# Attention by pairs of heads in the hybrid stages of a four-layer network on one NeuronCore

## The chip, the cores and the metric

The kernel runs as one program on one core of a Trainium2 chip. The metric is the device time of that core in microseconds. TensorE (PE in the profile) multiplies matrices and transposes, VectorE (DVE) and ScalarE (ACT) do elementwise work and move results out of PSUM, GpSimd (POOL) does a little, and SyncE (SP) issues the weight loads. Each engine executes its own queue strictly in the order in which the program was written.

## The reference

A sequence of 256 tokens of width 1024 passes eight stages: retention, dense FFN, stick-breaking attention, mixture of experts, and then twice a hybrid mixer followed by a convolutional FFN. Only the two hybrid mixers matter here. Cut to that:

```python
def hybrid_mixer(hn, w_in, conv_w, conv_b, gate_b, head_g, w_out):
    aq, ak, av, mq, mk, mv, mo, gates = split(hn @ w_in)      # 3 x 512, 4 x 512, 16 columns
    q, k = apply_rotary(heads(aq, 8)), apply_rotary(heads(ak, 8))
    attn = dilated_attention(q, k, heads(av, 8))              # 8 heads of 64: softmax(q k^T / 8 + bias) v
    mq, mk = split(silu(depthwise_conv_centred([mq, mk], conv_w, conv_b)))
    hm = mlstm(mq, mk, mv, gates) + flip(mlstm(flipped))      # 4 heads of 128, gates by scans over the tokens
    hm = hm * rsqrt(mean(hm * hm) + eps)
    return concat(attn, hm * head_g * sigmoid(mo)) @ w_out
```

The kernel folds the three dilation patterns into one additive bias (the log of how many patterns admit a pair of tokens), so each head is one softmax over 256 keys.

## The kernel before

All products are made in three passes of fp32r: each weight and activation is split in a high and a low part. A weight unit is a tile of 128 x 2048. It arrives by DMA (`raw`), ScalarE copies it to its high part `wh` (L83), VectorE subtracts to get the low part `wl` (L94). `W.advance()` issues the splits that buffers allow, five pairs at most; `W.get()` hands the oldest pair to the matmuls.

A hybrid stage (`hybrid`) goes through 14 input units, u = 0 to 13, and then four output units (`tail`). Each input unit is a projection of 48 matmuls (`mm3`, L200). Units 0 to 3 give queries and keys of the attention; `rotated` (L1012 on) turns them by angle on VectorE and `flip` (L1023 on) transposes them on TensorE, ScalarE copying the result to `qk`. Behind unit 3 `gating` computes the mLSTM gates with scans on VectorE (L981 to L999). Units 4 and 8 give attention values. Units 5, 6, 9 and 10 give mLSTM queries and keys, with a convolution of five taps (`conv` and `taps`: L1152 on ScalarE, eight instructions of L1159 on VectorE, a tanh L1162, `silu` L1166). Units 7 and 11 give mLSTM values, 12 and 13 the output gate.

The rest is tucked in behind the projections by the unit's number. Before the change, `attend(n)` handles one head per unit in u = 4 to 12: TensorE transposes the previous head's probabilities (L1041) and makes this head's scores (L1046), VectorE adds the bias and takes maxima (L1055), ScalarE exponentiates (L1061). `normalise` (L1065, L1067) follows the taps of the same unit, ahead of the mLSTM work in `todo` and ahead of `W.advance()`. `pv` (L1074) makes the value products of a pair of heads at u = 7, 9, 11, 13. `todo` places the mLSTM work: gate matrices (`gates`, L1089 and L1100), scores (`mscores`, L1106 and L1111), products and their norms (`mout`, L1127 to L1146).

PSUM has four single-bank buffers (`psP`) and two double-bank buffers (`psA`); an instruction that writes one waits until its last reader is done. The program's order is written by hand; no scheduler moves anything.

Of the kernel before, what the change touches and what calls it, by code (L numbers as in the profile page):

```python
# [10 lines left out]
F32 = mybir.dt.float32  # L11
# [4 lines left out]
AF = mybir.ActivationFunctionType  # L16
OP = mybir.AluOpType
PSUM = bass.MemoryType.PSUM

S, D = 256, 1024  # L20
# [105 lines left out]
def tok(t):  # L126
    return slice(t * 128, t * 128 + 128)
# [6 lines left out]
class Net:  # L134
# [805 lines left out]
    def hybrid(self, l, joint0):  # L940
        nc, tc, a, W = self.nc, self.tc, self.a, self.W
        with tc.tile_pool(name="h1", bufs=1) as p, tc.tile_pool(name="h2", bufs=2) as w:
# [66 lines left out]
            at = p.tile([128, 4, 2, S], F32, tag="at", name="at")  # L1009
            dn = {}  # L1010

            def rotated(ps):  # L1012

                x = w.tile([128, 2, 4, 2, 32], F32, tag="cv", name="ro")
                t1, t2 = (w.tile([128, 2, 8, 32], F32, tag="wk", name=n) for n in ("t1", "t2"))
                for t, i in ((t1, 0), (t2, 1)):
                    nc.vector.tensor_tensor(t, ps.rearrange("p t (h d) -> p t h d", d=32),  # L1017
                                            cs[:, :, i, None, :].to_broadcast([128, 2, 8, 32]), op=OP.mult)
                t1, t2 = (t.rearrange("p t (h i) d -> p t h i d", i=2) for t in (t1, t2))
                nc.vector.tensor_tensor(x[:, :, :, 0, :], t1[:, :, :, 0, :], t2[:, :, :, 1, :], op=OP.subtract)  # L1020
                nc.vector.tensor_tensor(x[:, :, :, 1, :], t2[:, :, :, 0, :], t1[:, :, :, 1, :], op=OP.add)
                return x.rearrange("p t h i d -> p t (h i d)")
# [8 lines left out]
                else:  # L1031
                    nc.scalar.activation(dst[0], ps, AF.Copy, scale=scale)

            def attend(n):

                A = self.psA()
                if n > 0:
                    x = at[:, (n - 1) % 2]
                    for jt in range(2):
                        for it in range(2):  # L1040
                            nc.tensor.transpose(A[:, 0, jt * S + it * 128:jt * S + it * 128 + 128], x[:, it, tok(jt)],  # L1041
                                                self.ident)
                r = slice(64 * (n % 2), 64 * (n % 2) + 64)
                ps = A[:, 1, :].rearrange("p (t s) -> p t s", t=2)
                for t in range(2 if n < 8 else 0):
                    nc.tensor.matmul(ps[:, t, :], lhsT=qk[r, 0, n // 2, tok(t)], rhs=qk[r, 1, n // 2, :],  # L1046
                                     start=True, stop=True)
                if n > 0:
                    nc.scalar.activation(at[:, 2 + (n - 1) % 2], A[:, 0, :].rearrange("p (t s) -> p t s", t=2), AF.Copy)
                if n == 8:  # L1050
                    return
                x = at[:, n % 2]
                m = self.small(2, "m")
                for t in range(2):
                    nc.vector.tensor_tensor_reduce(x[:, t, :], ps[:, t, :], bias[:, t, :], 1.0, -3e38, op0=OP.add,  # L1055
                                                   op1=OP.max, accum_out=m[:, t:t + 1])
                nm = self.small(2, "nm")
                nc.vector.tensor_scalar(nm, m, -1.0, None, op0=OP.mult)
                dn[n] = d = self.small(2, "dn")
                for t in range(2):  # L1060
                    nc.scalar.activation(x[:, t, :], x[:, t, :], AF.Exp, bias=nm[:, t:t + 1], accum_out=d[:, t:t + 1])  # L1061

            def normalise(n):
                d = dn.pop(n)
                nc.vector.reciprocal(d, d)  # L1065
                x = at[:, n % 2]
                nc.vector.tensor_tensor(x, x, d[:, :, None].to_broadcast([128, 2, S]), op=OP.mult)  # L1067

            def pv(c):
                ps = self.psP([128, S])  # L1070
                for j in range(2):
                    hd = slice((2 * c + j) * 64, (2 * c + j) * 64 + 64)
                    for jt in range(2):
                        nc.tensor.matmul(ps[64 * j:64 * j + 64, :], lhsT=v[:, jt, hd], rhs=at[:, 2 + j, jt, :],  # L1074
                                         start=(jt == 0), stop=(jt == 1), skip_group_check=True)
                self.split(ya[0][:, c, :], ya[1][:, c, :], ps)
# [38 lines left out]

            def mout(h):
                x = Dt.pop(h)
                A = [self.psP([128, 2, 129]) for _ in range(2)]

                def o(i, t):  # L1120
                    return A[i][:, t, :]

                def vv(t):
                    return va[:, t, h, :]

                def mm(out, l, r, start, stop):
                    nc.tensor.matmul(out, lhsT=l, rhs=r, start=start, stop=stop)  # L1127

                mm(o(0, 0), x[:, 0, 0:128], vv(0), True, True)
                mm(o(0, 1), x[:, 0, 128:256], vv(0), True, False)  # L1130
                mm(o(0, 1), x[:, 0, 256:384], vv(1), False, True)
                mm(o(1, 0), x[:, 1, 0:128], vv(0), True, False)
                mm(o(1, 0), x[:, 1, 128:256], vv(1), False, True)
                mm(o(1, 1), x[:, 1, 256:384], vv(1), True, True)
                d = self.sm.tile([128, 2, 2], F32, tag="den", name="den")
                for i in range(2):
                    nc.scalar.activation(d[:, i, :], A[i][:, :, 128], AF.Abs)
                    nc.vector.tensor_tensor(d[:, i, :], d[:, i, :], cols[:, 1, :, 32 * i + h], op=OP.max)
                r = self.sm.tile([128, 2, 2], F32, tag="rden", name="rden")
                nc.vector.reciprocal(r, d)  # L1140
                for t in range(2):
                    y = mix[:, t, tok(h)]
                    nc.vector.tensor_scalar(y, o(0, t)[:, :128], r[:, 0, t:t + 1], None, op0=OP.mult)  # L1143
                    nc.vector.scalar_tensor_tensor(y, o(1, t)[:, :128], r[:, 1, t:t + 1], y, op0=OP.mult, op1=OP.add)
                    j = w.tile([128, 128], BF, tag="junk1", name="junk1")
                    nc.scalar.activation(j, y, AF.Square, accum_out=ssq[:, 2 * h + t:2 * h + t + 1])  # L1146
# [18 lines left out]
            def silu(dst, th, y):  # L1165
                nc.vector.scalar_tensor_tensor(dst, th, 1.0, y, op0=OP.add, op1=OP.mult)  # L1166
# [5 lines left out]
            def mnorm():  # L1172
                nc.scalar.preload_act_table_set("sqrt_and_others")
                nc.scalar.activation(rs, ssq, AF.Sqrt, scale=4.0 / 128, bias=eps4)
                nc.vector.reciprocal(rs, rs)
# [20 lines left out]
            for u in range(14):  # L1196
                A = u in (5, 6, 9, 10)
                ps = next(first) if u < 4 else self.projA() if A else self.projB()
                if 0 < u < 5:
                    i = u - 1  # L1200
                    flip([qk[:, i % 2, i // 2 * 2:i // 2 * 2 + 2]], aq.pop(i), 0, 1.0 if i % 2 else 0.125)
                c = None
                if u < 4:
                    aq[u] = rotated(ps)
                elif A:
                    c = conv(ps, (u - 5) % 4, u // 9)
                elif u in (4, 8):
                    i = u // 8
                    nc.scalar.activation(v[:, :, i * 256:i * 256 + 256], ps, AF.Copy)
                elif u in (7, 11):  # L1210
                    i = u // 11
                    nc.scalar.activation(va[:, :, 2 * i:2 * i + 2, :128], ps.rearrange("p t (h d) -> p t h d", h=2),
                                         AF.Copy)
                else:
                    gated(u - 12, ps)
                if u in (7, 9, 11, 13):
                    pv((u - 7) // 2)
                if u == 5:
                    columns()
                if 4 <= u < 13:  # L1220
                    attend(u - 4)
                if A:
                    c = taps(*c)
                if 4 <= u < 12:
                    normalise(u - 4)
                if A:
                    silu(*c)
                if u == 3:
                    W.advance()
                for f in todo.get(u, []):  # L1230
                    f[0](*f[1:])
                if u == 4:
                    nc.scalar.preload_act_table_set("exp_and_others")
                if u not in (3, 13):
                    W.advance()
            mnorm()
            mfinal(0)
            joint = RmsNorm(self, p, w, a["mix_post_g"][l], a["ffn_pre_g"][l], "mqk")
# [325 lines left out]
```

## Time and profile before

| what | value |
|---|---|
| median of 3 runs | 2274.49 us (2272.34 to 2275.37) |
| profiled execution | 2273.95 us, its span 2272.2 us |
| PE busy | 2209.9 us, 97% of the span |
| DVE busy | 1709.9 us, 75% |
| ACT busy | 1374.3 us, 60% |
| 1585 to 1715 us (first hybrid stage) | PE 120.66, DVE 94.09, ACT 71.44 of 130 us |
| 1935 to 2070 us (second hybrid stage) | PE 127.65, DVE 99.94, ACT 74.32 of 135 us |

A matmul's record lasts until its last result leaves the array and overlaps the next one's, so a busy share of 97% for PE says little about whether it could go faster; its idle pieces and what ended them say more. Times of day in the rows are counted from the start of the span.

### The profile page before, as it was taken

To read this page: it belongs to the slowest core of one execution; us is meant where nothing else is said; L and a number is where in the kernel's file an instruction comes from. 1 tells how busy PE (TensorE), PEld (TensorE's weight loads), DVE (VectorE), ACT (ScalarE), POOL (GpSimd) and SP (SyncE) were. 2 spreads that over 40 slices of the span, in tenths; PEclk is the share of its full clock that TensorE was granted. 3 is DMA by queue.
4 is the path that set the end of the run, shared out by engine and by line. 5 is a ranking of instruction groups with operands and counts; after the bars stand their busy time and mean duration, and the time that the engine had idled before them with its cause. 6 is when DMAs were issued, how large, how long until landed. Compare 5 with 4: busy or idle time off the path is not lost. (4 is left out here: it accounts for less than half of the span.)

```text
span 2272.2 us, 31868 instructions
## 1 busy us (share of the span) xinstructions
PE 2209.9 (97%) x13077; PEld 1922.0 (85%) x13077; DVE 1709.9 (75%) x1671; ACT 1374.3 (60%) x1380; POOL 82.8 (4%) x86
## 2 busy tenths in 40 slices
PE   8999999998999999999999999997999999999998
PEld 8998998987888888878887788786888998888996
DVE  6565554647889888888887888987777974776972
ACT  4353543665777777777776777775556654555652
POOL 4100000010000000000000000200000000000000
PEclk9999999998999999999999999998999999999999
DMA  8444555537988899989988999994234554434551
GB/s 303 165 169 174 198 187 182 175 128 283 398 329 304 315 380 364 353 308 378 361 334 311 343 376 365 340 356 179 94 131 169 204 186 167 151 130 141 205 191 69
DMA packets 80074, 562.07 MB, mean 247 GB/s; under 512 B 9072, under 2 KB 9136, under 8 KB 13488
## 3 DMA queue, kind: packets, MB, share of 16 engines
q1 hardware_dynamic: 76464, 547.39, 65.5%
q0 software_dynamic: 3456, 12.55, 1.6%
q8 instruction: 105, 1.72, 0.3%
q14 instruction: 49, 0.40, 0.0%
HBM read 558.86 MB, written 1.05 MB: 246 GB/s over the span
## 5 line engine op out<-in xcount | busy, mean ns | idle before, releaser
L94 DVE TENSOR_TENSOR wl<-raw,wh 128x2048 fp32r<-128x2048 f32 x518 | 1189.3, 2300 | 314.5 <-ACT wh L83 312.9
L83 ACT ACTIVATE wh<-raw 128x2048 fp32r<-128x2048 f32 x518 | 991.3, 1916 | 393.4 <-PE pp L754 199.2
L200 PE MATMUL pp<-xh,wh 128*128 128x256 f32 x1360 | 388.9, 286 | 7.6 <-ACT wh L194 7.6
L200 PE MATMUL pp<-xh,wl 128*128 128x256 f32 x1360 | 385.9, 284 | 0.3 <-DVE wl L94 0.2
L200 PE MATMUL pp<-xl,wh 128*128 128x256 f32 x1360 | 383.9, 282 | 0.0
L200 PEld LDWEIGHTS pp<-xh,wh 128*128 128x128 f32 x1360 | 256.9, 189 | 9.4 <-ACT wh L194 8.2
L200 PEld LDWEIGHTS pp<-xl,wh 128*128 128x128 f32 x1360 | 259.1, 191 | 0.5 <-issue 0.5
L200 PEld LDWEIGHTS pp<-xh,wl 128*128 128x128 f32 x1360 | 257.2, 189 | 1.5 <-DVE wl L195 1.0
L200 PE MATMUL pp<-wh,xh 128*128 128x256 f32 x720 | 207.1, 288 | 5.3 <-DVE mix L1143 5.2
L200 PE MATMUL pp<-wh,xl 128*128 128x256 f32 x720 | 203.4, 282 | 0.0
L200 PE MATMUL pp<-wl,xh 128*128 128x256 f32 x720 | 203.0, 282 | 0.0
L754 PE MATMUL pp<-wh,xgh 128*128 128x512 f32 x448 | 179.6, 401 | 3.9 <-DVEq L831 3.9
L754 PE MATMUL pp<-wh,xh 128*128 128x512 f32 x448 | 179.4, 400 | 0.0
L754 PE MATMUL pp<-wl,xgh 128*128 128x512 f32 x448 | 177.0, 395 | 1.9 <-DVE wl L94 1.9
L754 PE MATMUL pp<-wl,xh 128*128 128x512 f32 x448 | 177.7, 397 | 0.7 <-DVE wl L94 0.7
L754 PE MATMUL pp<-wh,xl 128*128 128x512 f32 x448 | 177.6, 396 | 0.0
L754 PE MATMUL pp<-wh,xgl 128*128 128x512 f32 x448 | 177.1, 395 | 0.0
L200 PEld LDWEIGHTS pp<-wh,xh 128*128 128x128 f32 x720 | 137.0, 190 | 8.2 <-issue 6.1
L764 PE MATMUL pa<-wh,hh 128*128 128x512 f32 x448 | 142.0, 398 | 0.7 <-ACT hh L194 0.7
L764 PE MATMUL pa<-wh,hl 128*128 128x512 f32 x448 | 141.4, 397 | 0.0
L764 PE MATMUL pa<-wl,hh 128*128 128x512 f32 x448 | 141.3, 397 | 0.0
L200 PEld LDWEIGHTS pp<-wl,xh 128*128 128x128 f32 x720 | 136.9, 190 | 0.9 <-issue 0.7
(337 smaller groups left out, 3071.3 us busy)
## 6 DMA issues: line engine op xcount, KB each, us to landing
raw<-in_moe_w_in SPq DMA_DIRECT2D x224, 1024.0 KB, 5.3
raw<-in_moe_w_out SPq DMA_DIRECT2D x112, 1024.0 KB, 5.3
raw<-in_w_up SPq DMA_DIRECT2D x44, 1024.0 KB, 4.8
raw<-in_w_in SPq DMA_DIRECT2D x28, 1024.0 KB, 4.9
raw<-in_ret_w_in SPq DMA_DIRECT2D x23, 1024.0 KB, 5.0
raw<-in_ffn_w_in SPq DMA_DIRECT2D x22, 1024.0 KB, 4.9
raw<-in_w_down SPq DMA_DIRECT2D x22, 1024.0 KB, 4.8
raw<-in_ffn_w_out SPq DMA_DIRECT2D x11, 1024.0 KB, 4.8
```

What stands on the lines that cost most here:

```text
L83: self.nc.scalar.activation(h, self.rt[i][0], AF.Copy)
L94: self.nc.vector.tensor_tensor(l, r, h.bitcast(F32), op=OP.subtract)
L200: self.nc.tensor.matmul(out, lhsT=w, rhs=x, start=(i == 0), stop=(i == n - 1))
L754: nc.tensor.matmul(q, lhsT=x[:, k, :], rhs=ww[:, kk, :], start=(k == 0 and i == 0), stop=(k == KC - 1 and i == 2))
L764: nc.tensor.matmul(A[0][f], lhsT=x[:, k, :], rhs=ww[:, kk, half(f)], start=(s == 0 and k == 0 and i == 0), stop=(s == SL - 1 and k == 3 an ...
```

## The change

Attention goes by pairs of heads. `scores(c)` makes the scores of heads 2c and 2c+1, which lie in the lower and upper 64 partitions of `qk`, by matmuls that alternate between the two halves and write to the two banks of one `psA` buffer; then come four maxima, one negation, four exponentials. `normalise(c)` scales both heads at once. `turn()` transposes both (eight tiles) and copies them out in one instruction. Scores are made at u = 4, 7, 8, 11 (units without convolution), turns at 5, 8, 9, 12, value products at 6, 9, 10, 13; before, every unit from 4 to 12 had scores or transposes. `normalise` now comes last in its unit, behind `W.advance()`. The flips of rotated queries and keys come a unit later (u = 2 to 5), and the first two rotated tiles lie in `sg` for that. `mout(2)` accumulates in a `psA` buffer in place of two `psP` buffers. The probabilities have one buffer for a pair in place of two for single heads.

```diff
-            def rotated(ps):
-                x = w.tile([128, 2, 4, 2, 32], F32, tag="cv", name="ro")
+            def rotated(ps, n):
+                x = sg[:, n, :] if n < 2 else w.tile([128, 512], F32, tag="cv", name="ro")
...
-            def attend(n):
...
+            def scores(c):
+                A = self.psA().rearrange("p j (t s) -> p j t s", t=2)
+                for t in range(2):
+                    for j in range(2):
+                        r = slice(64 * j, 64 * j + 64)
+                        nc.tensor.matmul(A[:, j, t, :], lhsT=qk[r, 0, c, tok(t)], rhs=qk[r, 1, c, :],
+                                         start=True, stop=True)
+                m = self.small(4, "m")
+                for j in range(2):
+                    for t in range(2):
+                        nc.vector.tensor_tensor_reduce(at[:, j, t, :], A[:, j, t, :], bias[:, t, :], 1.0, -3e38,
+                                                       op0=OP.add, op1=OP.max,
+                                                       accum_out=m[:, 2 * j + t:2 * j + t + 1])
+                nm = self.small(4, "nm")
+                nc.vector.tensor_scalar(nm, m, -1.0, None, op0=OP.mult)
+                dn[c] = d = self.small(4, "dn")
+                for i in range(4):
+                    x = at[:, i // 2, i % 2, :]
+                    nc.scalar.activation(x, x, AF.Exp, bias=nm[:, i:i + 1], accum_out=d[:, i:i + 1])
+            def normalise(c):
+                d = dn.pop(c)
+                nc.vector.reciprocal(d, d)
+                x = at[:, :2].rearrange("p j t s -> p (j t) s")
+                nc.vector.tensor_tensor(x, x, d[:, :, None].to_broadcast([128, 4, S]), op=OP.mult)
+            def turn():
+                A = self.psA().rearrange("p j (t s) -> p j t s", t=2)
+                for j in range(2):
                     for jt in range(2):
                         for it in range(2):
+                            nc.tensor.transpose(A[:, j, jt, tok(it)], at[:, j, it, tok(jt)], self.ident)
+                nc.scalar.activation(at[:, 2:], A, AF.Copy)
...
+                if h == 2:
+                    wide = self.psA()
+                    A = [wide[:, i, :258].rearrange("p (t c) -> p t c", t=2) for i in range(2)]
...
-                if 0 < u < 5:
-                    i = u - 1
+                if 1 < u < 6:
+                    i = u - 2
...
-                if u in (7, 9, 11, 13):
-                    pv((u - 7) // 2)
+                if u in (6, 9, 10, 13):
+                    pv((6, 9, 10, 13).index(u))
                 if u == 5:
                     columns()
-                if 4 <= u < 13:
-                    attend(u - 4)
+                if u in (5, 8, 9, 12):
+                    turn()
+                head = {4: 0, 7: 1, 8: 2, 11: 3}.get(u)
+                if head is not None:
+                    scores(head)
                 if A:
-                    c = taps(*c)
-                if 4 <= u < 12:
-                    normalise(u - 4)
-                if A:
-                    silu(*c)
+                    silu(*taps(*c))
...
                 if u not in (3, 13):
                     W.advance()
+                if head is not None:
+                    normalise(head)
```

What stands in VectorE's queue from the end of the gate scans (L999) through unit 4 to the start of unit 5, before (`m` and `nm` are the maxima and their negation, `dn` the sums, `wl` a weight's low part, `gcols` the gate columns that unit 5 needs):

```order
L999 TENSOR_TENSOR tmp<-mix,M 36x256
L1055 ISA at,m<-pa,con 128x256
L1055 ISA m 128x1
L1055 ISA at,m<-pa,con 128x256
L1055 ISA m 128x1
L1058 TENSOR_SCALAR nm<-m 128x2
L1065 RECIPROCAL dn<-dn 128x2
L1067 TENSOR_TENSOR at<-at,dn 128x512
L94 TENSOR_TENSOR wl<-raw,wh 128x2048
L1007 COPY gcols<-pp 128x144
```

The same place in the changed kernel, from the last of the four maxima (L1046) on:

```order
L1046 ISA at,m<-pa,con 128x256
L1046 ISA m 128x1
L1050 TENSOR_SCALAR nm<-m 128x4
L94 TENSOR_TENSOR wl<-raw,wh 128x2048
L1058 RECIPROCAL dn<-dn 128x4
L1060 TENSOR_TENSOR at<-at,dn 128x1024
L1007 COPY gcols<-pp 128x144
```

The reciprocal and the normalise have moved from ahead of the low part of a weight to behind it; units 7, 8 and 11 have the same order.

ScalarE's queue in units 7 and 8 before (`va` and `v` are values copied out of PSUM, `at<-pa` the copy of turned probabilities, `at,dn` the exponentials, `wh` a weight's high part, `den` and `junk` belong to `mout`):

```order
L1212 ACTIVATE va<-pp 128x2x2x128
L194 ACTIVATE yh<-pp 128x256
L1049 ACTIVATE at<-pa 128x512
L1061 ACTIVATE at,dn<-at,nm 128x256 x2
L83 ACTIVATE wh<-raw 128x2048
L1209 ACTIVATE v<-pp 128x2x256
L1049 ACTIVATE at<-pa 128x512
L1061 ACTIVATE at,dn<-at,nm 128x256 x2
L1137 ACTIVATE den<-pp 128x2 x2
```

And in the changed kernel:

```order
L1217 ACTIVATE va<-pp 128x2x2x128
L1054 ACTIVATE at,dn<-at,nm 128x256 x4
L83 ACTIVATE wh<-raw 128x2048
L1214 ACTIVATE v<-pp 128x2x256
L1068 ACTIVATE at<-pa 128x1024
L1054 ACTIVATE at,dn<-at,nm 128x256 x4
L1142 ACTIVATE den<-pp 128x2 x2
```

Four exponentials stand ahead of each high part where two stood; one wide copy stands where there were two.

TensorE's queue in unit 8, from the last matmul of its projection to the first of unit 9's, before:

```order
L200 MATMUL pp<-wh,xl 128x256
L1041 MATMUL pa<-ident,at 128x128 x4
L1046 MATMUL pa<-qk 128x256 x2
L1127 MATMUL pp<-va,Dt 128x129 x6
L200 MATMUL pp<-xh,wh 128x256
```

And in the changed kernel:

```order
L200 MATMUL pp<-wh,xl 128x256
L1067 MATMUL pa<-ident,at 128x128 x8
L1041 MATMUL pa<-qk 128x256 x4
L1132 MATMUL pp<-va,Dt 128x129 x6
L200 MATMUL pp<-xh,wh 128x256
```

The turn of two heads and the scores of two heads stand between the projection and the mLSTM products of unit 8. The queues of SyncE and GpSimd are the same in both kernels.

## Rows read from the trace of the kernel before

**Rows 1.** PE waits, first hybrid stage: waiting <- awaited: us, times, longest.

```profile
PE pp L1028 <- DVE ro L1021: 4.4, 2, 3.0
PE pp L200 <- DVE mix L1143: 2.6, 1, 2.6
PE pa L1041 <- DVE at L1067: 2.4, 3, 1.6
```

**Rows 2.** Chain of waits, first hybrid stage: start us, us, engine, tile, line.

```profile
1618.66 0.43 DVE tmp L999
...
1620.39 1.08 ACT at L1061 x4
1621.49 1.28 ACT L1233
1622.79 1.92 ACT wh L83
...
1624.73 2.29 DVE wl L94
...
1627.24 0.33 DVE at L1055
...
1627.96 0.17 DVE nm L1058
1628.13 3.11 DVE cv L1159 x8
...
1633.21 1.81 ACT wh L83
...
1637.34 0.33 DVE at L1055
```

**Rows 3.** The same chain, later in that stage.

```profile
1670.84 0.07 ACT den L1137
...
1673.37 1.81 ACT wh L83
...
1697.47 5.93 PE pp L200 x48
...
1704.42 3.00 PE pa L239 x12
```

**Rows 4.** Chain of waits, second hybrid stage.

```profile
1961.00 0.43 DVE tmp L999
...
2048.51 3.00 PE pa L239 x12
```

**Rows 5.** PE timeline, unit 7: start us, us, line, form, count [idle].

```profile
1640.74 1.09 PE L1074 MATMUL pp<-at,v 128*64 128x256 f32 x8
1642.28 0.63 PE L1041 MATMUL pa<-ident,at 128*128 128x128 f32 x4 [0.45 <-DVE at L1067]
1642.84 1.13 PE L1046 MATMUL pa<-qk 64*128 64x256 f32 x4
1643.89 1.99 PE L1106 MATMUL pp<-mqk 128*128 128x256 f32 x8
```

**Rows 6.** PE timeline, the gate matmuls of unit 6.

```profile
1633.80 0.93 PE L1089 MATMUL pa<-M,con 4*128 4x256 f32 x8
...
1634.87 0.36 PE L200 MATMUL pp<-wh,xh 128*128 128x256 f32 x1
```

**Rows 7.** Line 1067, the normalise: count, ns least/median/most.

```profile
L1067 DVE TENSOR_TENSOR at<-at,dn x16: 691/692/694, 1621.7 to 2032.8; 128x512 f32<-128x512 f32 x16
```

**Rows 8.** PE timeline ahead of the first hybrid stage.

```profile
1583.87 1.46 PE L1303 MATMUL pa<-ident,z 128*128 128x128 f32 x6 [4.21 <-DVE z L1358]
```

**Rows 9.** Stretches: length, busy per engine, then PEclk, DMA share, GB/s.

```profile
1583.90:1587.40 3.50, 3.50 (x17) 3.47 (x18) 1.96 (x3) 2.20 (x3) 2.19 (x6) 0.52 0.26 69
1606.20:1612.00 5.80, 5.80 (x48) 5.60 (x49) 5.77 (x6) 2.40 (x2) 0.00 (x0) 1.00 0.79 294
2040.10:2043.00 2.90, 2.90 (x19) 2.90 (x20) 1.92 (x8) 1.05 (x8) 0.00 (x0) 0.72 0.65 274
```

More of the change, by code (lines that the diff above doesn't have):

```diff
@@ L1010, in hybrid @@
             dn = {}
-            def rotated(ps):
-                x = w.tile([128, 2, 4, 2, 32], F32, tag="cv", name="ro")
+            def rotated(ps, n):
+                x = sg[:, n, :] if n < 2 else w.tile([128, 512], F32, tag="cv", name="ro")
+                x = x.rearrange("p (t h i d) -> p t h i d", t=2, h=4, i=2)
                 t1, t2 = (w.tile([128, 2, 8, 32], F32, tag="wk", name=n) for n in ("t1", "t2"))
@@ L1032, in flip @@
                     nc.scalar.activation(dst[0], ps, AF.Copy, scale=scale)
-            def attend(n):
-                A = self.psA()
-                if n > 0:
-                    x = at[:, (n - 1) % 2]
+            def scores(c):
[17 more added lines that the diff above has]
+                    nc.scalar.activation(x, x, AF.Exp, bias=nm[:, i:i + 1], accum_out=d[:, i:i + 1])
@@ L1039, in attend @@
+            def normalise(c):
[6 more added lines that the diff above has]
+                for j in range(2):
                     for jt in range(2):
                         for it in range(2):
-                            nc.tensor.transpose(A[:, 0, jt * S + it * 128:jt * S + it * 128 + 128], x[:, it, tok(jt)],
-                                                self.ident)
@@ L1043, in attend @@
[L1043 to L1067, printed above, removed]
+                            nc.tensor.transpose(A[:, j, jt, tok(it)], at[:, j, it, tok(jt)], self.ident)
+                nc.scalar.activation(at[:, 2:], A, AF.Copy)
             def pv(c):
@@ L1117, in mout @@
                 x = Dt.pop(h)
-                A = [self.psP([128, 2, 129]) for _ in range(2)]
+                if h == 2:
+                    wide = self.psA()
+                    A = [wide[:, i, :258].rearrange("p (t c) -> p t c", t=2) for i in range(2)]
+                else:
+                    A = [self.psP([128, 2, 129]) for _ in range(2)]
                 def o(i, t):
@@ L1203, in hybrid @@
                 if u < 4:
-                    aq[u] = rotated(ps)
+                    aq[u] = rotated(ps, u)
                 elif A:
```

## The prediction

> **What bounds the kernel now.** I read four views: the waits of TensorE over one hybrid stage, the chain of waits through that stage, TensorE's timeline around its small matmuls, and the granted clock in stretches. Only the two hybrid stages differ, some 130 us each; the rest of the program has the same instructions in the same order, so I cost it at nothing.
>
> The waits show how little TensorE stands still in the first hybrid stage: 4.4 us for rotated queries and keys, 2.6 us for the products of the gated heads, 2.4 us for normalised probabilities [rows 1]. That looks like some 9 us to be had. The chain says otherwise. From the gate scans on (their last step ends at 1618.66 + 0.43 = 1619.09) it hardly touches TensorE: it goes exponentials, table load, high half of the next weights (wh, ScalarE), low half (wl, VectorE), maxima, convolution taps, tanh, gate exponentials, wh and wl again [rows 2]. VectorE and ScalarE hand each other work, each in its written order, and TensorE runs just behind. A weight split stands in this chain not because TensorE lacks weights (unit 8's are split before the scans), but because later instructions stand behind it in VectorE's queue. So the reader is to ask of each moved instruction: what is ahead of it in its queue?
>
> I measure each stage from the end of the scans to the first matmul of the output projection: 1704.42 - 1619.09 = 85.3 us in the first [rows 2, 3], and 2048.51 - 1961.43 = 87.1 us in the second [rows 4].
>
> **The change part by part.** *Flips a unit later.* They take TensorE's 4.4 us of waiting away [rows 1]. But the scans come at the end of VectorE's queue of rotations and splits, and VectorE is full there (5.77 of 5.80 us busy) [rows 9]. That queue is the same before and after, and what feeds it comes earlier, not later, so the scans end at 1619.1 as now. Worth 0; the 4.4 us are spent again at the next wait. Bounds: -1 to +1 us.
>
> *Scores of two heads in the two row halves.* One head's scores take 1643.89 - 1642.84 = 1.05 us, from start to the next group. The value products, eight records in the two column halves, take 1.09 us, whereas eight records over the full array with as many columns take 1.99 us [rows 5]: halves run beside each other. I take 1.05 us for a pair (with no overlap 2.1), if row halves do as column halves do, so 4 x 1.05 = 4.2 us less of TensorE a stage. On the path this counts only where scores are waited for.
>
> *One normalise a pair.* Half the width takes 0.69 us [rows 7]; wl, the same operation at twice the width, takes 2.29 us [rows 2]. Between them, 0.69 + 1.6 / 3 = 1.22, and with its reciprocal 1.3 us (bounds 0.8 and 2.4).
>
> *Where the normalise stands.* This decides. Before, it came ahead of the gate work and of the split; now each unit with scores issues maxima, exponentials, gate work, wh, wl and only then the normalise. The next unit's turn waits for it, and behind the turn wait, on TensorE, the gates or mLSTM matmuls and the next projection; on ScalarE, behind the copy of the turned pair, the tanh or exponentials.
>
> The durations for the sum: a maximum 0.34, its negation 0.21 with its issue, two exponentials 1.08 so four 2.1, table load 1.28, wh 1.9 (1.8 when queued directly behind other work), wl 2.3 [rows 2]. Eight taps to the start of wh are 1633.21 - 1628.13 = 5.1, so taps to the end of wl 5.1 + 1.8 + 2.3 = 9.2 [rows 2]. Abs, division and norm sums of one mLSTM head are 1673.37 - 1670.84 = 2.5 [rows 3]. A projection is 5.9 [rows 3]. A turn of four tiles takes 1642.84 - 1642.28 = 0.56; eight tiles I take at 1.0 (bounds 0.6 and 1.1); the products of one mLSTM head are twelve records of about the same width, 1.4, of two heads 2.7 [rows 5]. The gate matmuls take 1634.87 - 1633.80 = 1.1 [rows 6].
>
> The new chain, unit by unit:
> Unit 4: four maxima and negation 1.6, exponentials 2.1, table 1.3, wh 1.9, wl 2.3, normalise 1.3: 10.5.
> Unit 5: gate columns and taps to wl, 0.2 + 9.2 = 9.4. TensorE's own way, turn 1.0, gates 1.1, projection 5.9, value product 1.0 and its split 0.4, is 9.4 too.
> Unit 6: split of the value product 0.35 and 9.2: 9.55.
> Unit 7: maxima and negation 1.6, exponentials 2.1, wh 1.8, wl 2.3, normalise 1.3: 9.1 (the products with the gates lie beside the exponentials and wh).
> Unit 8: turn 1.0 and scores 1.05 on TensorE first, then unit 7's list with one head's sums (2.5 and 0.2 for their first step) in it: 13.85.
> Unit 9: 0.35, taps to wl 9.2, one head's sums 2.5: 12.05.
> Unit 10 as unit 6: 9.55. Unit 11 as unit 7: 9.1.
> Unit 12 and 13: turn 1.0, two heads' products 2.7, projection 5.9, value product 1.0: 10.6.
> Sum: 10.5 + 9.4 + 9.55 + 9.1 + 13.85 + 12.05 + 9.55 + 9.1 + 10.6 = 93.7 us.
>
> So +8.4 us in the first stage and +6.6 us in the second, +15.0 together. The convolution units get shorter by what left them (before, 1627.24 to the next unit's maxima is 10.1 us against 9.4 and 9.55). Units 4, 7, 8 and 11 get longer by more: in each, the whole split of a weight, 1.8 + 2.3 us, now stands between scores and turn.
>
> *mout(2) in the other PSUM pair.* It frees the last projection from its 2.6 us wait [rows 1]; that is inside the 10.6. Two maxima, reciprocals and negations saved lie in the sum too.
>
> *The clock.* TensorE's new waits are long: in unit 5 from about 1620.4, when the gate columns are out, to the normalise at 1619.1 + 10.5 = 1629.6, so 9 us; in unit 8 some 3 (unit 7's maxima start 1.9 us after its scores, since unit 6 holds VectorE for 9.95 us from its value product on and TensorE needs 8.05 for gates, projection and scores; then 9.1 against 2.0 of mLSTM scores and a projection); in unit 9 some 3.5 (11.8 from scores to normalise, against 1.4 + 5.9 + 1.0); in unit 12 some 4.5 (30.7 for units 9 to 11 against 26.2 of TensorE). After a wait of 4.21 us TensorE was granted 0.52 of its clock for 3.5 us, that is 1.2 of 2.4 GHz, and 0.72 over 2.9 us at the last projection of the second stage, where the 2.6 us wait of the first stage has its like; after a 3.0 us wait it stayed at 1.00 [rows 1, 8, 9]. A stretch at the lower level of 3.5 us loses 1.7 us of work. I count it for the two longest waits, both on the path (unit 5, where TensorE's way equals the chain, and unit 12): 3.4 us a stage, 6.8 in all; bounds 0 and, with unit 8 and a second stretch after the 9 us wait, 6.8 a stage.
>
> The profiled execution took 2273.95 us (span 2272.2 and 1.75 around it), 0.5 under the median of 2274.49. 2273.95 + 15.0 + 6.8 = 2295.8 us.
>
> **The rivals.**
> *The clock holds.* The same chain, but the waits leave the clock alone, as the 3.0 us wait did [rows 1, 9]: 2273.95 + 15.0 = 2289. Against it, 9 us is twice the longest wait in the rows.
>
> *Every wait costs clock.* Units 5, 8 and 12 on the path at 1.7 us each, and a second stretch after the longest: 6.8 a stage, 2273.95 + 15.0 + 13.6 = 2302.5. Unit 9 has slack behind it, since unit 10's taps wait for VectorE. For it: two of three waits in the rows dropped the clock. The Trainium skill, page "TensorE: Matmul & The Clock Gate", section "HAM oscillation", says that bursts of matmuls parted by such waits each start over at half rate; by that rule this rival is the outcome. The trace agrees after 4.21 us [rows 8, 9], and not after 3.0 us.
>
> *Faster: TensorE's order sets the pace.* If the normalise were done when TensorE comes to the turn, the waits of 2.6 and 2.4 us and 4.2 us of scores would go: 9.2 us a stage, 2273.95 - 18.4 = 2255.5; with the 4.4 us of rotation too, 2247. The place is the turn of units 8, 9 and 12. Between scores and turn TensorE has a projection and 1.4 to 2.4 us of small products, 7.3 to 8.3 us; the link from scores to normalise takes 9.1 us even when VectorE is free at once. It decides from a link below 7.3 us, so 1.8 us shorter, for example a split that is not in the way. In favour: before, the wait for probabilities was only 2.4 us over eight heads. Against: there the normalise stood ahead of the split.
>
> *It does not do what it says:* the row halves run one after the other. Then unit 8 alone pays, 1.05 us a stage: 2298. The overlap of column halves speaks against it [rows 5].
>
> **How the numbers follow.** What a measurement can tell from no change is about 0.2%, 4.5 us. Forecast, with its clock losses between one and three a stage: 0.50. Clock holds: 0.17. Every wait costs clock: 0.15. Row halves in series: 0.04. Faster: 0.09. Gains and losses cancel within 4.5 us: 0.05. So slower 0.86, same 0.05, faster 0.09. The range from 2281 to 2304 holds all but the faster and equal cases and a little at the top, near 0.8; its lower end allows the chain to be 4 us a stage shorter than summed (a normalise at its lower bound, a smaller second stage).
>
> **What would show it.** Right: scores of a pair, eight records, in about 1.1 us; no wait for rotations; four waits of the turn for the normalise in each stage, of some 9, 3, 3.5 and 4.5 us; half-clock stretches behind the first and the last; scans ending where they end now, and the output projection 8 to 13 us later. Wrong: turns that start without a wait, or scans that end much earlier, which would mean that the rotations did hold the path. If the unit 5 wait is there but the rest are under 1 us each, the sum fails in units 7 to 11.

## The result and the profile after

The changed kernel took 2308.72 us (median of 4 runs, 2307.02 to 2311.77) against 2274.01 us (4 runs, 2272.34 to 2275.37): a ratio of 1.0156, 95% interval 1.0143 to 1.0168, or 34.7 us slower. The forecast was 2295.8 us, slower by 22, and its range ended at 2304. Direction and place were right; the size was not.

First TensorE's waits in the changed kernel, over the first hybrid stage (waiting <- awaited: us, times, longest):

```profile
PE pa L1067 <- DVE at L1060: 20.8, 4, 9.4
PE pp L1006 <- ACT qk L1033: 1.5, 1, 1.5
```

The waits for rotations (4.4 us), for the mLSTM products (2.6 us) and for single heads [rows 1] are gone. In their place stand four waits of the turn for the pair's normalise, 20.8 us together; the second stage has four again, 20.4 us.

The chain of waits through units 4 to 6 of that stage (start us, us, engine, tile, line):

```profile
1619.23 2.08 ACT at L1054 x8
...
1621.32 1.28 ACT L1237
...
1622.61 1.92 ACT wh L83
...
1624.56 2.29 DVE wl L94
...
1626.97 1.24 DVE at L1060
...
1628.34 1.94 PE pa L1067 x8
1630.28 2.13 PE pa L1090 x10
1632.41 7.92 PE pp L200 x48
...
1642.23 3.13 DVE cv L1164 x8
```

This answers to [rows 2]. There, taps followed the low half of the split directly. Here the normalise (L1060) follows it, and behind the normalise the chain goes onto TensorE: turn, gates and the whole projection. Look at the last of these: 7.92 us, where a projection took 5.93 [rows 3].

Stretches of the changed kernel: length, busy time of PE, PEld, DVE, ACT and POOL, then PEclk, DMA share, GB/s. The first two are the whole stages from the end of the scans to the output projection. Then come unit 5's stretch and what follows it, and the stretches at the turns of units 8, 9 and 12 (from the start of unit 8's turn, and from some 1 us after the start of the other two). The last is unit 9's again, in the second stage.

```profile
1617.50:1719.94 102.44, 80.64 (x589) 73.60 (x589) 59.53 (x138) 51.04 (x110) 1.10 (x2) 0.87 0.27 93
1976.97:2081.39 104.42, 83.97 (x601) 77.03 (x600) 59.89 (x138) 51.08 (x110) 1.10 (x2) 0.85 0.26 91
...
1628.30:1637.00 8.70, 8.66 (x42) 8.04 (x43) 5.29 (x11) 4.81 (x7) 0.00 (x0) 0.50 0.27 109
1637.00:1660.00 23.00, 19.91 (x159) 18.19 (x158) 14.10 (x32) 10.05 (x20) 0.00 (x0) 1.00 0.27 92
1660.70:1664.40 3.70, 3.63 (x16) 2.56 (x16) 0.00 (x0) 1.02 (x1) 0.00 (x0) 0.54 0.64 266
1677.50:1681.50 4.00, 4.00 (x25) 3.72 (x25) 3.02 (x7) 2.60 (x6) 0.00 (x0) 0.57 0.43 176
1708.90:1713.10 4.20, 4.20 (x26) 4.20 (x25) 0.95 (x5) 1.26 (x3) 0.00 (x0) 0.61 0.41 174
2036.00:2043.00 7.00, 7.00 (x38) 6.51 (x37) 4.52 (x14) 3.13 (x8) 0.00 (x0) 0.53 0.28 116
```

The stages lasted 102.4 and 104.4 us, against 85.3 and 87.1 [rows 2 to 4]. That is 17.1 and 17.3 us more, 34.4 together: the whole loss lies between these two marks. (In the first stage the scans themselves ended 1.6 us earlier than before, at 1617.5; in the second they came as long after the first stage's end as before.) And at all four turns the granted clock falls to about half (1.2 of 2.4 GHz), in unit 5 for 8.7 us of work.

### The profile page after: what moved, and what is told of

Same layout as the page of the kernel before. It is cut to its first block, busy times and chain, and to the rows that moved or that the text cites. A ratio compares the mean times of both kernels' runs of the same rounds, so it can differ in the third digit from the quotient of the medians.

```text
span 2305.2 us, 31806 instructions
## 1 busy us (share of the span) xinstructions
PE 2216.2 (96%) x13077; PEld 1931.9 (84%) x13077; DVE 1707.1 (74%) x1647; ACT 1374.7 (60%) x1372; POOL 86.1 (4%) x86
## 5 line engine op out<-in xcount | busy, mean ns | idle before, releaser
L94 DVE TENSOR_TENSOR wl<-raw,wh 128x2048 fp32r<-128x2048 f32 x518 | 1189.4, 2300 | 328.3 <-ACT wh L83 327.5
```

Of the source, the lines that this page charges most:

```text
L94: self.nc.vector.tensor_tensor(l, r, h.bitcast(F32), op=OP.subtract)
```

## The experiments

| run | us | ratio (95%) | stages, us |
|---|---|---|---|
| the change | 2308.7 | 1.0156 (1.0143 to 1.0168) | 102.4, 104.4 |
| normalise ahead of the split | 2270.9 | 0.9988 (0.9979 to 0.9998) | 85.4, 85.6 |
| useless matmuls ahead of four turns | 2291.7 | 1.0084 (1.0068 to 1.0101) | 94.7, 95.0 |
| the flips alone | 2274.5 | 1.0003 (0.9993 to 1.0012) | 88.4, 85.5 |
| split early | 2270.8 | 0.9987 (0.9977 to 0.9996) | 86.7, 84.0 |
| before, normalise behind the split | 2323.1 | 1.0215 (1.0201 to 1.0229) | 111.4, 111.5 |
| useless matmuls in unit 5 only | 2303.0 | 1.0125 (1.0109 to 1.0140) | 102.5, 101.3 |
| useless matmuls in units 8, 9, 12 | 2298.3 | 1.0110 (1.0095 to 1.0126) | 98.5, 98.8 |
| normalise first, useless matmuls | 2271.0 | 0.9990 (0.9981 to 0.9999) | 83.9, 85.4 |
| the same, unit 5's taps first | 2264.0 | 0.9956 (0.9943 to 0.9970) | 81.7, 80.9 |
| taps first, no useless matmuls | 2270.5 | 0.9986 (0.9977 to 0.9995) | 83.8, 85.8 |
| taps first, 22 useless matmuls | 2263.4 | 0.9954 (0.9940 to 0.9967) | 81.6, 80.6 |

Ratios are to the kernel before on the same chip. The single stages vary by 2 to 3 us from profile to profile (the flips alone gave 88.4 and 85.5, where before had 85.3 and 87.1), so a few microseconds of one stage settle nothing.

**The place of the normalise.** One edit to the changed kernel: the same call, ahead of the table load and the split.

```diff
                 for f in todo.get(u, []):
                     f[0](*f[1:])
+                if head is not None:
+                    normalise(head)
...
                     W.advance()
-                if head is not None:
-                    normalise(head)
```

> The changed kernel with the normalise of a pair ahead of the unit's weight split instead of behind it; nothing else differs. Theory (queue): the turns wait because the normalise stands behind wh and wl. Then three of the four waits of a stage go, only the last turn may wait some 3 us, a stage from the end of the scans to the output projection takes 82 to 87 us instead of 102.5, and the time is 2272 us (2264 to 2280). Rival (pairs): two heads at a time make the link from scores to turn too long by themselves; then the turns still wait for 3 us or more each and the time stays above 2293 us.

It took 2270.85 us: 37.9 us less than the change, 3.1 less than before. TensorE's waits over its first stage:

```profile
PE pa L1067 <- DVE at L1060: 6.4, 3, 4.0
PE pp L1006 <- ACT qk L1033: 1.6, 1, 1.6
PE pp L1107 <- DVE mqk L1171: 1.1, 1, 1.1
```

20.8 us of waiting for the normalise have become 6.4. The time is as expected, the waits are not quite: one of some 3 us was to be left, and there are two, 4.0 us in unit 5 and 2.2 in unit 12. Pairs, row halves, moved flips and the wide `mout(2)` are all still in it, so none of them makes the loss.

**The same from the other side.** The kernel before, with only its one-head normalise put behind the split:

```diff
-                if 4 <= u < 12:
-                    normalise(u - 4)
                 if A:
                     silu(*c)
...
                     W.advance()
+                if 4 <= u < 12:
+                    normalise(u - 4)
```

> The kernel before, with its one-head normalise moved behind the unit's weight split and nothing else changed: no pairs, no row halves, flips where they were. Theory (the place in the queue alone makes the loss): 2300 us (2288 to 2312). Each unit's link from scores to the next turn then holds turn 0.5, scores 0.5, maxima 0.9, the unit's gate work or exponentials, the split 4.1 and a normalise 0.8: 9 + 12 + 12 + 8 + 10.7 + 14.5 + 12 + 8 + 10 = 96 us from scans to output projection, 11 us a stage more than before, and 0 to 7 us a stage of half clock on top. Rival (the loss comes from making pairs, and the place matters only with them): 2274 us (2270 to 2280).

2323.12 us, 49.8 more than before: the place alone makes a loss, with no pairs at all. It came out above the expected 2288 to 2312. TensorE's waits over the first stage, then two stretches that begin at turns:

```profile
PE pa L1041 <- DVE at L1067: 14.3, 8, 3.5
```

```profile
1628.60:1636.50 7.90, 7.86 (x33) 6.41 (x34) 4.17 (x14) 1.69 (x5) 0.00 (x0) 0.50 0.42 133
1643.50:1650.00 6.50, 6.47 (x29) 5.17 (x30) 3.14 (x11) 1.69 (x5) 0.00 (x0) 0.54 0.51 164
```

Eight waits in this stage, none above 3.5 us, and behind the two looked at here 14.4 us at about half clock. Over the whole stage the granted clock was 0.85, where the same stage before had 1.00. So the up to 7 us a stage that I allowed for the clock were probably too little again; how the 111.4 us divide between chain and clock was not taken apart.

**The clock.** The changed kernel with matmuls whose product is thrown away, written into the turn's own buffer ahead of its transposes: 72 in unit 5, 28 in units 8, 9 and 12. They keep TensorE busy where it waits; the queues of the other engines stay as they are.

```diff
-            def turn():
+            def turn(fill):
                 A = self.psA().rearrange("p j (t s) -> p j t s", t=2)
+                for i in range(fill):
+                    nc.tensor.matmul(A[:, 0, 0, :], lhsT=self.xh[:, i % KC, tok(0)], rhs=self.xh[:, i % KC, :],
+                                     start=True, stop=True)
...
-                    turn()
+                    turn(72 if u == 5 else 28)
```

> The changed kernel with matmuls that serve nothing ahead of each turn, written to the turn's own PSUM buffer before it is overwritten: 72 in unit 5 (8.5 us at full clock), 28 (3.3 us) in units 8, 9 and 12, so that TensorE is busy while it would wait for the normalise; the computation is unchanged. Theory (clock): half-clock stretches behind the waits cost some 8 us a stage; then the granted clock stays at 1.00, a stage takes 93 to 96 us instead of 102.5, and the time is 2293 us (2288 to 2299). Rival (clock hidden): the chain over VectorE and ScalarE is 102 us long whatever TensorE's clock, and the time is 2304 to 2311 us.

2291.70 us: useless work made the kernel 17.0 us faster. The two stages of this run, columns as above:

```profile
1618.82:1713.51 94.69, 90.97 (x745) 84.75 (x745) 59.17 (x138) 50.60 (x110) 1.10 (x2) 1.00 0.28 101
1970.55:2065.58 95.03, 92.36 (x758) 85.95 (x756) 59.16 (x139) 50.55 (x110) 1.10 (x2) 1.00 0.29 101
```

With the clock held at 1.00 the stages last 94.7 and 95.0 us. The predicted sum for the chain was 93.7. VectorE's last step in a unit (the normalise L1060, in units 6 and 10 the low part L94) marks where the time goes. In the chain of this run's first stage, for units 4, 6, 7, 8, 10 and 11 (start us, us):

```profile
1628.31 1.24 DVE at L1060
...
1646.58 2.29 DVE wl L94
...
1656.82 1.24 DVE at L1060
...
1670.94 1.23 DVE at L1060
...
1691.50 2.29 DVE wl L94
...
1701.74 1.24 DVE at L1060
```

The same marks in the changed kernel, where the first is the normalise at 1626.97 shown above:

```profile
1649.16 2.29 DVE wl L94
...
1659.40 1.24 DVE at L1060
...
1675.14 1.24 DVE at L1060
...
1696.36 2.29 DVE wl L94
...
1706.60 1.24 DVE at L1060
```

From the end of each mark to the end of the next, starting at the end of the scans and ending at the output projection, in us:

| units | forecast for the chain | useless matmuls, clock at 1.00 | changed kernel |
|---|---|---|---|
| 4 | 10.5 | 10.7 | 10.7 |
| 5 and 6 | 18.95 | 19.3 | 23.3 |
| 7 | 9.1 | 9.2 | 9.2 |
| 8 | 13.85 | 14.1 | 15.75 |
| 9 and 10 | 21.6 | 21.6 | 22.3 |
| 11 | 9.1 | 9.2 | 9.2 |
| 12 and 13 | 10.6 | 10.5 | 12.1 |

With the clock held every part of the sum comes out within 0.4 us. The last two columns differ only behind a turn: by 3.9 us behind unit 5's, 1.6 behind unit 8's, 0.7 behind unit 9's and 1.6 behind unit 12's. By the same marks the second stage has 3.5, 1.4, 1.9 and 2.7 us.

Where the half clock bites is seen in TensorE's timeline of unit 5 (start us, us, line, form, count, [idle]); first the changed kernel, then the run with useless matmuls:

```profile
1628.34 1.94 PE L1067 MATMUL pa<-ident,at 128*128 128x128 f32 x8 [9.43 <-DVE at L1060]
1630.21 1.66 PE L1090 MATMUL pa<-M,con 4*128 4x256 f32 x8
...
1632.17 0.56 PE L200 MATMUL pp<-xh,wh 128*128 128x256 f32 x1
...
1640.25 1.09 PE L1075 MATMUL pp<-at,v 128*64 128x256 f32 x8
```

```profile
1629.68 1.06 PE L1070 MATMUL pa<-ident,at 128*128 128x128 f32 x8 [0.62 <-DVE at L1060]
1630.68 0.93 PE L1093 MATMUL pa<-M,con 4*128 4x256 f32 x8
...
1631.74 0.36 PE L200 MATMUL pp<-xh,wh 128*128 128x256 f32 x1
...
1637.67 1.09 PE L1078 MATMUL pp<-at,v 128*64 128x256 f32 x8
```

From the turn to the value product: 1640.25 - 1628.34 = 11.91 us in the one, 1637.67 - 1629.68 = 7.99 in the other. The half clock takes 3.9 us here, all of it seen in the table for units 5 and 6, so unit 5's way over TensorE is on the path.

**Which waits cost it.** The same edit with `turn(72 if u == 5 else 0)`, and its complement with 28 at units 8, 9 and 12 only.

> The changed kernel with 72 useless matmuls of 128x256 ahead of unit 5's turn alone, none ahead of the turns of units 8, 9 and 12. Theory (the 9 us wait of unit 5 makes half of the clock loss, the three waits of 4 us the other half): 2300 us (2296 to 2304), no half clock from 1620 to 1640, half clock behind the other turns as in the changed kernel. Rival (the first wait makes all of it, as its stretch is the longest): 2292 us, like the run with useless matmuls ahead of all four turns. Second rival (the first wait's loss has slack behind it, so the others make all): 2307 us.

> The changed kernel with 28 useless matmuls ahead of the turns of units 8, 9 and 12 and none ahead of unit 5's: the complement of the run that had them in unit 5 alone (it won 5.7 us, all four turns together 17.0). Theory (what half clock costs adds up over the waits): 2308.7 - 11.3 = 2297.4 us (2294 to 2301). Rival (the long stretch behind the 9 us wait carries over into the later waits, so that it is lost either way): 2302 us or more. Second rival (the stretch of unit 5 has slack behind it once the later ones are gone): 2292 us.

2303.03 us (5.7 saved) and 2298.30 us (10.4 saved): 16.1 together, 17.0 with all four at once. So the losses add up within the noise, and both times lie in their theories' ranges. How they divide is known only roughly: the times of the changed kernel spread from 2307.0 to 2311.8 us, those of the run with unit 5's cover alone from 2300.5 to 2305.1. By these medians unit 5's wait makes a third of the loss, by the marks above 7.4 of 17.1 us. Two sentences of the first expectation failed. The useless matmuls themselves ran at half clock for a while (1621.7 to 1625.1 us at 0.50 in the first stage). And the other turns did not look as in the first stage of the changed kernel; behind unit 9's there was

```profile
1674.40:1681.00 6.60, 6.52 (x33) 5.90 (x33) 4.25 (x11) 3.18 (x7) 0.00 (x0) 0.50 0.35 144
```

6.6 us at 0.50, where the changed kernel had 4.0 us at 0.57 in its first stage and 7.0 us at 0.53 in its second. The three waits were 3.6, 3.7 and 3.7 us long. The length of a stretch at the lower level thus isn't fixed by its own wait.

**The flips.** Flips and tile buffers of the change, put into the kernel before:

```diff
-                if 0 < u < 5:
-                    i = u - 1
+                if 1 < u < 6:
+                    i = u - 2
```

> The kernel before with one part of the change alone: flips of rotated queries and keys a unit later, with the first two in sg. Theory (VectorE full up to the scans): the 4.4 us of waits go and are spent again later, scans end at the same distance from the start of the stage, 2274 us (2271 to 2277). Rival (rotations on the path): 3 to 9 us less, 2265 to 2271 us.

2274.47 us, ratio 1.0003 (0.9993 to 1.0012): nothing, as costed. TensorE's 4.4 us of waiting for rotations went, but VectorE was full up to the scans; they ended at 1618.1 us, where before had 1619.1, and the time did not move.

**Toward a faster order.** First, the unit's split issued ahead of its gate work, so that nothing but the normalise stands between exponentials and turn:

```diff
+                more = 3 < u < 13 and W.split_h()
...
-                    silu(*taps(*c))
+                    c = taps(*c)
+                if more:
+                    W.split_l()
+                if A:
+                    silu(*c)
+                if head is not None:
+                    normalise(head)
```

> The changed kernel with the weight split pulled out of the chain between VectorE and ScalarE: wh is issued on ScalarE right behind the unit's first copies, wl on VectorE behind taps or maxima, and the normalise behind that, ahead of the gate and mLSTM work. Theory (queue): the order of wh and wl in the queues makes the chain; with wh beside the taps a convolution unit is 6.5 us on VectorE, less than TensorE's 8 to 10, TensorE sets the pace, and the time is 2255 us (2246 to 2264). Rival (something else is late, buffers or the normalise): as the run with the normalise first, 2266 us or more.

2270.79 us: a miss, no better than the normalise first alone. The waits over its first stage show what was late instead:

```profile
PE pa L1067 <- DVE at L1060: 5.6, 1, 5.6
PE pp L1107 <- DVE mqk L1171: 2.7, 2, 2.1
PE pp L1006 <- ACT qk L1033: 1.5, 1, 1.5
```

In unit 4 the high part of the split now stood ahead of the exponentials and the low part ahead of the normalise (one wait of 5.6 us, and half clock behind it); the mLSTM scores came to wait 2.7 us for `silu`, where the version with the normalise first had 1.1.

Then two edits to the version with the normalise first: useless matmuls ahead of two turns, and unit 4's split and table load moved into unit 5, with its low half behind the taps.

```diff
                     c = conv(ps, (u - 5) % 4, u // 9)
+                    if u == 5:
+                        nc.scalar.preload_act_table_set("exp_and_others")
+                        W.split_h()
...
-                    turn()
+                    turn({5: 34, 12: 18}.get(u, 0))
...
-                    silu(*taps(*c))
+                    c = taps(*c)
+                    if u == 5:
+                        W.split_l()
+                    silu(*c)
...
-                if u == 4:
-                    nc.scalar.preload_act_table_set("exp_and_others")
-                if u not in (3, 13):
+                if u not in (3, 4, 13):
```

Useless matmuls alone (the third piece):

> The changed kernel with the normalise ahead of the gate work and the split, and useless matmuls ahead of two turns: 34 in unit 5, 18 in unit 12. Theory (in units 5 to 7 of that version VectorE and ScalarE set the pace, so half clock there costs nothing; only unit 12's turn, projection and value product are on the path): 2268 us (2265 to 2271). Rival (TensorE's half clock in unit 5 is on the path too): 2263 us or less.

Both:

> As the run sent beside it (normalise first, useless matmuls ahead of the turns of units 5 and 12), and unit 4's weight split and the table load moved: the table and the high half behind unit 5's convolution copies, the low half behind unit 5's taps, so that the taps no longer wait for exponentials, table load and a whole split. Theory (the chain of VectorE and ScalarE from the scans to unit 6's maxima sets the pace; TensorE's own way comes next, 2.7 to 3.2 us a stage shorter): 2262 us (2257 to 2267). Rival (it returns at the next wait, as the early split did): 2268 us, as without it.

The moved split alone:

> The version with normalise first and unit 5's taps ahead of unit 4's split, without any useless matmul. Theory (TensorE now sets the pace from unit 5 on, so what half clock its 4 us wait in unit 5 brings is lost, some 2 to 4 us a stage, against 1.6 us a stage by which the useless matmuls ran on after the normalise, and 1.7 us at unit 12): 2267 us (2263 to 2271). Rival (slack hides the half clock, the useless matmuls only cost): 2261 us.

2271.04, 2263.95 and 2270.49 us, against 2270.85 with neither: each alone gains nothing (the first missed its 2268), both together 6.9 us. From the end of the scans to unit 6's first tap the first stage took 19.04 us with neither, 19.05 with the useless matmuls alone, 19.07 with the moved split alone and 16.9 with both. The stretch behind unit 5's turn in the version without useless matmuls shows one side of it:

```profile
1624.20:1632.50 8.30, 8.30 (x41) 7.65 (x42) 6.79 (x12) 7.46 (x9) 0.00 (x0) 0.50 0.20 66
```

With the taps early, unit 6 waits for TensorE at half clock: from the turn to the value product it took 11.7 us there and 8.0 with both edits. With the clock held and the taps late, unit 6's taps (1637.3 us) follow directly on the low part of unit 5's split, which ends at 1637.1. Two limits stood beside each other, and taking away one showed the other. Last, 34 useless matmuls had held the first stage's turn back until 1.6 us after it could have started, so 22 were tried:

> The same with 22 useless matmuls in unit 5 (34 ran until 1.6 us after the normalise) and 18 in unit 12. Theory (TensorE's order sets the pace from unit 5's turn to the output projection, so a turn 1.3 us earlier counts in full): 2264.0 - 2.6 = 2261.4 us (2259 to 2264). Rival (VectorE and ScalarE set the pace again, or the shorter cover drops the clock): 2264 to 2267 us.

2263.41 us, not told apart from 2263.95. In the first stage the turn did come 1.5 us earlier, but a wait of 1.2 us was left, and behind it stands

```profile
1626.20:1630.00 3.80, 3.80 (x23) 3.80 (x22) 3.80 (x6) 3.80 (x8) 0.00 (x0) 0.55 0.02 4
```

so half clock took back there what the earlier turn gave: unit 6's taps began at 1635.6 us in both versions. Both versions beat the kernel before by 0.45% and the change by 2%.

## Why the prediction was wrong

*What bounds the kernel.* Right: the chain of VectorE and ScalarE, not TensorE's small idle. The rival in which TensorE sets the pace did not come. A normalise with no split in the way is the first experiment, and even that gave 3.1 us and not 18; the normalise still came 4.0 us late in unit 5 and 2.2 in unit 12.

*Flips worth 0.* Right for the time, 2274.47 against 2273.99 us; the scans of the first stage ended 1.6 us earlier in the changed kernel, a little over the bound of 1. *Row halves.* Right: eight records of a pair's scores take 1649.28 - 1648.21 = 1.07 us, as one head's four did [rows 5]. *Normalise.* 1.24 us against 1.22. The changed kernel's timeline of units 7 to 12 has both the scores and the waits:

```profile
1648.21 1.13 PE L1041 MATMUL pa<-qk 64*128 64x256 f32 x8
1649.28 1.99 PE L1107 MATMUL pp<-mqk 128*128 128x256 f32 x8
1660.77 1.75 PE L1067 MATMUL pa<-ident,at 128*128 128x128 f32 x8 [3.85 <-DVE at L1060]
1662.44 2.08 PE L1041 MATMUL pa<-qk 64*128 64x256 f32 x8
...
1676.52 1.06 PE L1067 MATMUL pa<-ident,at 128*128 128x128 f32 x8 [3.68 <-DVE at L1060]
...
1707.97 1.19 PE L1067 MATMUL pa<-ident,at 128*128 128x128 f32 x8 [3.85 <-DVE at L1060]
```

*The four waits.* Forecast some 9, 3, 3.5 and 4.5 us; the rows have 9.4, 3.85, 3.7 and 3.85. *The chain.* 93.7 us forecast; with the clock held at 1.00, 94.7 and 95.0, so 2.3 us short over both stages. Its parts fit one by one, so this was not luck.

*The step that failed* is the clock's term, "1.7 us of work" for "the two longest waits", 3.4 us a stage. The run with useless matmuls measures it: 17.0 us, 8.5 a stage, above even the upper bound of 6.8. Two things were wrong in it. I counted two of four waits; all four dropped the clock. Unit 8's, which I had only in the bound, cost 1.6 and 1.4 us in the two stages by the marks. Unit 9's, which I took to be hidden by slack, was hidden only in part: 0.7 and 1.9. And I gave the 9 us wait a stretch as short as the one behind 4.21 us [rows 8, 9], with a second one only in the bound: it ran at 0.50 for 8.7 us after work had resumed and cost 3.9 and 3.5 us where I had 1.7. Unit 12's 1.7 was right in the first stage (1.6) and short in the second (2.7).

So 10.2 us of the miss of 12.9 are the clock, 2.7 the chain and the bases of the two sums. The rival "every wait costs clock" had the mechanism. At 2302.5 us it is still 6 short: 3.4 of that because it too used 1.7 us for each stretch and left unit 9 out, the rest with the chain. The Trainium skill, page "TensorE: Matmul & The Clock Gate", section "HAM oscillation", says that a burst behind such a wait starts over at half rate; the trace agrees in units 5 and 8 of the first stage, whose turns took 1.94 and 1.75 us where a turn with the clock held took 1.06. In units 9 and 12 the turn itself still ran at or near the full clock (1.06 and 1.19 us), and the clock fell just behind it. I had given that rule 15 in 100, with a single wait that spoke against it.

Open: why the stretch in unit 5 is the long one. It is as long behind a 4.0 us wait (8.3 us at 0.50 in the version with the taps first) as behind 9.4 us. What is particular there is that TensorE did only four small matmuls between one wait of 1.5 us and the other; whether that or the small matmuls behind the turn prolong it was not tried. Nor is it known when a wait leaves the clock alone: in the kernel before, the last projection, behind a wait of 2.6 us in either stage, ran at 1.00 in the first (1697.5 to 1703 us) and began at 0.72 in the second [rows 1, 9].

## What to carry to other kernels

Before you merge or move a step on an engine that executes in order, list what its new place puts ahead of it: here one call, a line below a weight split, was worth 38 us, and all the rest of the change together a gain of 3. When a change makes TensorE wait, cost the half clock behind every wait, and not one fixed price for the longest: here the half clock behind a wait cost between 0.7 and 3.9 us. When an edit that takes away a limit gains nothing, try it together with the edit for the limit beside it: twice nothing made 7 us here.

## What the runs showed of the hardware

Matmuls whose results nobody reads saved 17.0 us of 2308.7, by keeping the granted clock at 1.00 in both stages, in place of waits of up to 9.4 us; where another engine's chain was the limit (2271.04 against 2270.85) they saved nothing. And the length of a wait doesn't order the stretch behind it: 8.7 us at 0.50 behind 9.4 us, 8.3 us at 0.50 behind 4.0, 4.0 us at 0.57 and 7.0 us at 0.53 behind 3.7, 3.8 us at 0.55 behind a wait of 1.2 us.
